# One layer's top-k search: two query tiles searched one by one, first query operands made earlier

## The chip, the cores and the metric

The kernel runs on one core of one Trainium2 chip. The time is device microseconds of one execution; the median of three runs before the change is 1343.3 us (1337.26 to 1343.76).

## The reference

One decoder layer for a sequence of 1024 tokens with 1024 channels, in float32. A conditioning vector gives shift, scale and gate; the modulated input is projected into attention (8 heads of 64), an indexer and pooling channels. The part that matters here is the sparse attention: for each query the indexer scores every earlier token, the 256 best are kept, and attention runs over those alone.

```python
logits = einsum('bqhd,bsd->bqhs', iq, ik) * (IDX_DIM ** -0.5)
score = einsum('bqh,bqhs->bqs', w, relu(logits))
score = where(causal, score, -inf)
_, idx = lax.top_k(score, k_sel)            # k_sel = 256
...
s = einsum('bqhd,bqkhd->bhqk', q, kg) * (HEAD_DIM ** -0.5)
p = softmax(where(valid, s, -inf)); o = einsum('bhqk,bqkhd->bqhd', p, vg)
...
x = layer_norm(ALPHA * x + gate1 * (concat([attn, pool_out]) @ w_o))
x = layer_norm(ALPHA * x + gate2 * swiglu(x * (1 + scale2) + shift2))
```

## The kernel before

Queries come in 8 tiles of 128; tile i sees 128·(i+1) keys. The stages follow one another: modulation; indexer projections; the score stage (`lg` on PE, `relu` on ACT, weighted sums into `score_X`); a list of 24 `groups` of projections (8 of u, then 8 of k, then 8 of v, one 1024-deep product each); attention; W_o and layer norm; the feed-forward part with products `gu` and `dn`.

Nobody gathers. For tiles 2 to 7 the 256th largest score of each query is found by bisection on the bits of the scores, and all other scores get a large negative bias in `score_X`, which attention adds. (Tiles 0 and 1 have at most 256 keys and need no search.) `bisect(tiles, cols, on_act)` is that search as a generator of small pieces: a count and a rewriting of the scores into 16-bit `keys` on DVE; 15 steps on the high bits; a middle part on DVE; 16 steps on the low bits; then a final part on DVE (equality, count, a scan that settles ties, and the bias), of some ten instructions per tile, after which the tile is `biased`. On ACT a step is one pass per tile (`ACTIVATE junk…<-keys…,cols…`, a Sign with a sum over the row, and an `ACTIVATION_READ_ACCUMULATOR`), and then four small instructions on POOL on the columns `cols`, which hold one value per query and tile: they make the next candidate, for all tiles of the search at once. The next pass of that search waits for them.

The work order is written by the program: each engine's `Queue` (line 158 is its call, so nearly all rows have that line) keeps a planned clock, and before it issues an instruction `fill` puts search pieces in front of it, as long as a piece ends, on that clock, within `SLACK[queue]` us behind the time at which the instruction could start. Streams opened earlier come first. While `pinned` holds, the order of DVE, ACT and POOL is kept as written. ACT searches `TILES_A`, tiles 3 and 2 as one stream and 7 and 6 as another; DVE searches tiles 5 and 4.

Attention goes by head groups g (0 to 3), pairs of heads, and in each pair tile 2g+1 and then 2g. For a tile `q_make` turns the roped queries (loaded back by `q_load` into `qraw`, transposed on PE as `qT`) into operands in the buffer `qab`: four ACT copies and two DVE subtractions, for a high and a low part. A unit is: scores `s` on PE into one of two PSUM buffers (`psB`), on DVE the bias and row maximum (the custom instruction, `sm_H<-s,score_X`, printed as `ISA` in the orders below), the exponential on ACT, the normalising on POOL, transposes `pT` on PE, copies of those on ACT and DVE, and `o` on PE. The exponential loads an ACT table once (`ACT_TABLE_LOAD`). The buffer areas of SBUF have one letter each (X, V, W, H, T, C, K, R), which ends every name in the profile: `qab_H` lies in area H. V holds values and the pooling data.

Of the kernel before, what the change touches and what calls it, by code (L numbers as in the profile page):

```python
# [12 lines left out]
F32R = mybir.dt.float32r  # L13
# [20 lines left out]
BIG = 1.0e30  # L34
NEG = -3.0e38
NOT_TAKEN = -(2.0 ** 100)
TILES_A = ([3, 2], [7, 6])
TILES_V = [5, 4]
PIN = "VAG"
W_POOL = (1, 3)  # L40
# [7 lines left out]
MODS = (12, 2)  # L48
Q_AT = (((0, 0), (1, 0)), ((0, 0), (1, 0)), ((1, 0), (2, 0)))
WARM = 66  # L50
SLACK = {"V": 0.5, "A": 1.5}
SYNC = 0.06
UPDATE = "G"
POOL_AT = 3
# [123 lines left out]
def decoder_layer_kernel(  # L178
# [22 lines left out]
    def buf(where, off, n, name, dt=F32):  # L201
        return nc.alloc_sbuf_tensor_at(f"{name}_{where}{off}", [P, n], dt, offset=area[where] + 4 * off).ap()
# [59 lines left out]
    def raw_slot():  # L262
        n_raw[0] += 1
        return RAW[(n_raw[0] - 1) % 3]
# [286 lines left out]
    def q_transpose(src):  # L551
        pt = psA("qT")
        for pr in range(4):
            T.transpose(pt[:, pr * P : (pr + 1) * P], src[:, pr * P : (pr + 1) * P], ident)
        return pt
# [56 lines left out]

    kA = buf("X", 4224, 448, "keysA")
    colsA = buf("X", 4672, 128, "colsA")
    junk7 = buf("X", 4800, 512, "junk").bitcast(BF16)
    kD = buf("T", 0, 960, "keysD")
    k4 = buf("T", 960, 320, "keys4")
    k5 = buf("T", 1280, 384, "keys5")
    junkA = buf("X", 6528, 512, "junkA").bitcast(BF16)
    junkB = buf("X", 7040, 256, "junkB").bitcast(BF16)  # L620
    colsD = buf("X", 8576, 64, "colsD")
    keys = {2: kA[:, 0:192], 3: kA[:, 192:448], 4: k4, 5: k5, 6: kD[:, 0:448], 7: kD[:, 448:960]}
    keys = {i: kw.bitcast(I16) for i, kw in keys.items()}
# [3 lines left out]
    def bisect(tiles, cols, on_act):  # L627
# [3 lines left out]
        cntc, kp, sg, cand, pr, M, ng, th, ib, thr, ahead = (col(q) for q in range(11))  # L631
        flip = ib.bitcast(I16)[:, 0:nt]
        kv = {i: keys[i] for i in tiles}
        own = (junkA if 7 in tiles else junkB) if on_act else junk7

        def trash(i):
            return own[:, 0 : P * (i + 1)]
# [100 lines left out]
    def open_stream(*a):  # L738
        pinned.update(PIN)
        b = bisect(*a)  # L740
        streams.append([T.t, next(b), b])
        times.fill = fill
# [40 lines left out]
    for i in range(2, NT):  # L783
        if i == 4:
            open_stream(TILES_A[0], colsA[:, 0:64], True)
        n = P * (i + 1)
        qa, ql = iq_ops(i)
        sc = score(i)
        for pr in range(4):
            pe, po = psB("lg"), psB("lg")  # L790
            scores_pair(pe, po, qa, ql, pr, ikE, ikO, n)
            q_piece()
            if pr == 1 and i + 1 < NT:
                nxt = q_transpose(iq_raw(i + 1))
            for e, pp in ((0, pe), (1, po)):
                h = 2 * pr + e
                rr = rrr[:, (n_rr[0] % 4) * 1024 : (n_rr[0] % 4) * 1024 + n]
                n_rr[0] += 1
                A.activation(rr, pp[:, 0:n], AF.Relu, scale=0.125)
                w1 = wq8[:, i * 8 + h : i * 8 + h + 1]  # L800
                if h == 0:
                    V.tensor_scalar(sc, rr, w1, 0.0, ALU.mult, ALU.add)
                else:
                    V.scalar_tensor_tensor(sc, rr, w1, sc, ALU.mult, ALU.add)
            next(gate_steps, None)
            if pr == 1 and i + 1 < NT:
                q_operands(nxt, *iq_ops(i + 1))
            if pr == 2 and qpend:
                q_flush(1)
                q_evac(*qpend.pop(0))  # L810
        dg = sc[:, n - P : n]
        G.affine_select(dg, dg, pattern=[[-1, P]], compare_op=ALU.is_ge, fill=NEG, base=0, channel_multiplier=1)
    open_stream(TILES_V, colsD, False)
    open_stream(TILES_A[1], colsA[:, 64:128], True)


    SP.dma_start(pscale, pscale_in)
# [90 lines left out]
    def at_(slot, f):  # L908
        late.setdefault(slot, []).append(f)
# [27 lines left out]

    PAIRS = (0, 6, 8, 14, 16)
    held, pair = {}, None
    for n_, (kind, a, b) in enumerate(groups):  # L940
        if n_ in PAIRS:
            pb = psB("pair")
# [26 lines left out]
            at_(nd, lambda a=a, pp=pp: v_take(a, pp))  # L969
        if n_ == 20:  # L970
            at_(n_, lambda: gate_fin(GR, macc, 0, raw_slot()))
        for f in late.pop(n_, []):
            f()
    last = len(groups)
    pinned.clear()


    stat = [buf("X", 8448, 128, "stat")]
# [4 lines left out]
        n_st[0] = (o + n) % 128 if o + n + n <= 128 else 0  # L983
        return stat[0][:, o : o + n]

    ptb = [[buf("H", (2 * s_ + e) * 2048, 2048, "pT").rearrange("p (j q) -> p j q", j=8) for e in (0, 1)] for s_ in (0, 1)]
    smr = buf("H", 8192, 6144, "sm")
    qabh = buf("H", 14336, 1536, "qab", F32R)
    qabw = [buf("W", 6144 - 2048 * i, 1536, "qab", F32R) for i in (0, 1)]
    qabv = [buf("V", 5120 + i * 1536, 1536, "qab", F32R) for i in (0, 1)]  # L990
    qab = {1: qabh, 0: qabw[0], 3: qabw[1], 2: qabw[0], 5: qabh, 4: qabv[0], 7: qabv[1], 6: qabh}

    qops = {}

    qraw = [buf("C", 768, 512, "qraw"), buf("X", 7552, 512, "qraw")]

    def q_load(i):
        raw = qraw[i % 2]
        SP.dma_start(raw, q_d[i])
        return raw  # L1000

    def q_make(i, raw, pt=None):
        b = qab[i]
        qops[i] = (b[:, 0:1024], b[:, 1024:1536])
        q_operands(pt if pt is not None else q_transpose(raw), *qops[i])

    for s_ in (last, last + 1):
        if s_ == last:
            qr = {i: q_load(i) for i in (1, 0)}
            qp = {i: q_transpose(qr[i]) for i in (1, 0)}  # L1010
        for f in late.pop(s_, []):
            f()
    assert not late, late
    for i in (1, 0):
        q_make(i, qr[i], qp[i])

    def cat_slot(g):
        return WS[g]
# [581 lines left out]
```

## Time and profile before

| | |
|---|---|
| three runs | 1343.76, 1343.3, 1337.26 us |
| profiled execution | 1340.45 us, of it the span 1338.5 us |
| mean granted TensorE clock | 0.95 |
| busy | PE 91%, DVE 75%, POOL 45%, ACT 44% |
| stages, roughly | scores to 186 us, projections 186 to 343, attention 343 to 570, W_o and feed-forward to the end |

A row of the timeline is: start, duration, engine, line, operation, out<-in, shapes, xcount of consecutive ones, and in brackets the idle time before it with what released it. A row of the waits is: who waited for whom, us in total, times, longest. A row of grouped instructions is: line, engine, operation, out<-in, shapes, xcount, then total us and mean ns of one, then the idle time before them with its releasers.

### The profile page before, as it was taken

To read this page: it belongs to the slowest core of one execution; us is meant where nothing else is said; L and a number is where in the kernel's file an instruction comes from. 1 tells how busy PE (TensorE), PEld (TensorE's weight loads), DVE (VectorE), ACT (ScalarE), POOL (GpSimd) and SP (SyncE) were. 2 spreads that over 40 slices of the span, in tenths; PEclk is the share of its full clock that TensorE was granted. 3 is DMA by queue.
4 is the path that set the end of the run, shared out by engine and by line. 5 is a ranking of instruction groups with operands and counts; after the bars stand their busy time and mean duration, and the time that the engine had idled before them with its cause. 6 is when DMAs were issued, how large, how long until landed. Compare 5 with 4: busy or idle time off the path is not lost. (4 is left out here: it accounts for less than half of the span.)

```text
span 1338.5 us, 15961 instructions
## 1 busy us (share of the span) xinstructions
PE 1219.7 (91%) x5570; PEld 958.7 (72%) x5570; DVE 1006.4 (75%) x1685; ACT 592.4 (44%) x1103; POOL 606.0 (45%) x624
## 2 busy tenths in 40 slices
PE   7978997989586849999799999999999999999996
PEld 6655676768454526788677888888888888888875
DVE  6898789889766778467887767576767767676688
ACT  2345754667888956427533223232323223232321
POOL 1393584675344536315663414152342414242557
PEclk8999999989677978999899999999999999999998
DMA  9540020221103431420121011120101112110112
GB/s 337 213 162 31 16 92 19 95 68 44 48 24 118 142 111 64 169 84 1 47 79 63 32 63 63 50 76 33 63 32 64 42 53 70 57 63 32 63 48 110
DMA packets 24997, 101.79 MB, mean 76 GB/s; under 512 B 3411, under 2 KB 3411, under 8 KB 20566
## 3 DMA queue, kind: packets, MB, share of 16 engines
q1 hardware_dynamic: 24918, 100.78, 21.5%
q8 instruction: 44, 0.72, 0.2%
q14 instruction: 35, 0.29, 0.1%
HBM read 92.38 MB, written 8.40 MB: 75 GB/s over the span
## 5 line engine op out<-in xcount | busy, mean ns | idle before, releaser
L158 POOL TENSOR_TENSOR wraw_R<-wraw_R 128x512 f32<-128x512 f32 x44 | 60.1, 1366 | 178.3 <-DVE wblk_T L158 51.3
L158 POOL TENSOR_TENSOR wraw_W<-wraw_W 128x512 f32<-128x512 f32 x44 | 59.5, 1353 | 169.3 <-DVE wblk_V L158 63.8
L158 DVE TENSOR_TENSOR res_X<-res_X,dn 128x512 f32<-128x512 f32 (+1 forms) x145 | 97.4, 680 | 50.9 <-PE dn L158 50.9
L158 PE MATMUL gu<-hr_H,wblk_T 128*128 128x512 f32 (+1 forms) x552 | 125.7, 384 | 3.4 <-ACT stage_W L158 2.6
L158 PE MATMUL gu<-hr_H,wblk_V 128*128 128x512 f32 (+1 forms) x552 | 125.5, 382 | 3.3 <-ACT gtmp_V L158 1.8
L158 PE MATMUL gu<-hr_H,wblk_W 128*128 128x512 f32 (+1 forms) x552 | 125.4, 383 | 0.0
L158 PE MATMUL pj<-ws_W,hT_H 128*128 128x512 f32 x456 | 117.9, 406 | 2.4 <-DVE const_C L158 1.6
L158 PEld LDWEIGHTS gu<-hr_H,wblk_T 128*128 128x128 f32 x552 | 101.7, 191 | 23.7 <-ACT stage_W L158 2.9
L158 PEld LDWEIGHTS gu<-hr_H,wblk_V 128*128 128x128 f32 x552 | 101.0, 189 | 24.0 <-ACT gtmp_V L158 2.0
L158 PEld LDWEIGHTS gu<-hr_H,wblk_W 128*128 128x128 f32 x552 | 101.8, 191 | 19.6
L158 PEld LDWEIGHTS pj<-ws_W,hT_H 128*128 128x128 f32 x456 | 84.5, 191 | 27.6 <-issue 10.2
L158 DVE TENSOR_TENSOR utmp_X<-utmp_X,gu 128x512 f32<-128x512 f32 x88 | 58.2, 682 | 33.5 <-PE gu L158 32.4
L158 DVE TENSOR_TENSOR gtmp_V<-gtmp_V,gu 128x512 f32<-128x512 f32 (+1 forms) x96 | 59.1, 638 | 28.2 <-PE gu L158 28.2
L158 POOL TENSOR_TENSOR colsA_X<-colsA_X 128x2 f32<-128x2 f32 x124 | 40.0, 323 | 80.6 <-ACT junkA_X L158 52.4
L158 POOL TENSOR_SCALAR sm_H<-sm_H,stat_X 128x256 f32<-128x256 f32 (+7 forms) x64 | 53.3, 846 | 50.6 <-DVE stat_X L158 40.1
L158 PE MATMUL dn<-wblk_T,act_W 128*128 128x512 f32 (+1 forms) x294 | 75.1, 385 | 0.0
L158 ACT ACTIVATE junkA_X<-keysD_T,colsA_X 128x1024 bf16<-128x1024 uint16 (+3 forms) x62 | 67.7, 1091 | 15.5 <-POOL colsA_X L158 15.1
L158 PE MATMUL dn<-wblk_V,act_W 128*128 128x512 f32 x288 | 74.4, 389 | 0.0
L158 ACT ACTIVATE act_W<-gtmp_V 128x512 fp32r<-128x512 f32 x40 | 25.3, 633 | 94.9 <-DVE gtmp_V L158 92.9
L158 PE MATMUL gu<-hr_H,wblk_R 128*128 128x512 f32 (+1 forms) x276 | 64.1, 381 | 3.4 <-DVE hr_H L158 3.0
L158 DVE TENSOR_SCALAR_CACHE_REDUCE junk_X<-keys_T,colsD_X 128x768 int16<-128x768 int16 (+1 forms) x64 | 64.3, 1005 | 2.0
L158 PEld LDWEIGHTS dn<-wblk_T,act_W 128*128 128x128 f32 x294 | 54.6, 188 | 11.1
(276 smaller groups left out, 2869.6 us busy)
## 6 DMA issues: line engine op xcount, KB each, us to landing
wm_K<-in_wma_dram SPq DMA_DIRECT2D x16, 512.0 KB, 9.6
raw_R<-in_wmc_dram SPq DMA_DIRECT2D x16, 512.0 KB, 3.7
wraw_R<-in_wg_dram SPq DMA_DIRECT2D x6, 1024.0 KB, 4.7
wraw_R<-in_wd_dram SPq DMA_DIRECT2D x6, 1024.0 KB, 4.8
wraw_W<-in_wup_dram SPq DMA_DIRECT2D x6, 1024.0 KB, 4.8
wraw_R<-in_wup_dram SPq DMA_DIRECT2D x5, 1024.0 KB, 4.8
wraw_W<-in_wg_dram SPq DMA_DIRECT2D x5, 1024.0 KB, 4.8
wraw_W<-in_wd_dram SPq DMA_DIRECT2D x5, 1024.0 KB, 4.8
```

Of the source, the lines that this page charges most:

```text
L158: ins_ = f(*a, **k)
```

## The change

- Tiles 7 and 6 are no longer one ACT search of two columns but two searches, tile 6's opened ahead of tile 7's, and both ahead of DVE's. Each has its own `cols` (tile 7's is `colsE_T`), its own `junk`, and four POOL instructions per step of its own.
- ACT's slack is 0.3 us up to the end of the score stage, 2.5 from there to the end of the projections, and 0.3 behind it; it was 1.5 all along.
- The queries of tile 1 are loaded at group 17 and made into operands behind group 20, those of tile 0 at 21 and behind 23, both into area V. Before, they were loaded, transposed and made behind the last group, into H and W. The other tiles' places in H, W and V change with them.

```diff
--- before.py
+++ after.py
@@ -34,7 +34,7 @@
 BIG = 1.0e30
 NEG = -3.0e38
 NOT_TAKEN = -(2.0 ** 100)
-TILES_A = ([3, 2], [7, 6])
+TILES_A = ([3, 2], [6], [7])
 TILES_V = [5, 4]
 PIN = "VAG"
 W_POOL = (1, 3)
@@ -48,7 +48,7 @@
 MODS = (12, 2)
 Q_AT = (((0, 0), (1, 0)), ((0, 0), (1, 0)), ((1, 0), (2, 0)))
 WARM = 66
-SLACK = {"V": 0.5, "A": 1.5}
+SLACK = {"V": 0.5, "A": 0.3}
 SYNC = 0.06
 UPDATE = "G"
 POOL_AT = 3
@@ -612,12 +612,12 @@
 
     kA = buf("X", 4224, 448, "keysA")
     colsA = buf("X", 4672, 128, "colsA")
-    junk7 = buf("X", 4800, 512, "junk").bitcast(BF16)
+    junks = {2: buf("X", 5184, 256, "junk"), 4: buf("X", 4800, 384, "junk"), 6: buf("X", 7040, 448, "junk"),
+             7: buf("X", 6528, 512, "junk")}
...
-    junkA = buf("X", 6528, 512, "junkA").bitcast(BF16)
-    junkB = buf("X", 7040, 256, "junkB").bitcast(BF16)
+    colsE = buf("T", 1664, 64, "colsE")
     colsD = buf("X", 8576, 64, "colsD")
     keys = {2: kA[:, 0:192], 3: kA[:, 192:448], 4: k4, 5: k5, 6: kD[:, 0:448], 7: kD[:, 448:960]}
     keys = {i: kw.bitcast(I16) for i, kw in keys.items()}
@@ -631,7 +631,7 @@
         cntc, kp, sg, cand, pr, M, ng, th, ib, thr, ahead = (col(q) for q in range(11))
         flip = ib.bitcast(I16)[:, 0:nt]
         kv = {i: keys[i] for i in tiles}
-        own = (junkA if 7 in tiles else junkB) if on_act else junk7
+        own = junks[min(tiles)].bitcast(BF16)
 
         def trash(i):
             return own[:, 0 : P * (i + 1)]
@@ -810,8 +810,10 @@
                 q_evac(*qpend.pop(0))
         dg = sc[:, n - P : n]
         G.affine_select(dg, dg, pattern=[[-1, P]], compare_op=ALU.is_ge, fill=NEG, base=0, channel_multiplier=1)
+    SLACK["A"] = 2.5
+    open_stream(TILES_A[1], colsA[:, 64:128], True)
+    open_stream(TILES_A[2], colsE, True)
     open_stream(TILES_V, colsD, False)
-    open_stream(TILES_A[1], colsA[:, 64:128], True)
 
 
     SP.dma_start(pscale, pscale_in)
@@ -937,6 +939,28 @@
 
     PAIRS = (0, 6, 8, 14, 16)
     held, pair = {}, None
+    qr = {}
+    ptb = [[buf("H", (2 * s_ + e) * 2048, 2048, "pT").rearrange("p (j q) -> p j q", j=8) for e in (0, 1)] for s_ in (0, 1)]
+    smr = buf("H", 8192, 6144, "sm")
+    qabh = buf("H", 14336, 1536, "qab", F32R)
+    qabw = buf("W", 6144, 1536, "qab", F32R)
+    qabv = [buf("V", 5120 + i * 1536, 1536, "qab", F32R) for i in (0, 1)]
+    qab = {1: qabv[0], 0: qabv[1], 3: qabh, 2: qabw, 5: qabv[0], 4: qabv[1], 7: qabh, 6: qabv[0]}
+
+    qops = {}
+
+    qraw = [buf("X", 5504, 512, "qraw"), buf("X", 7552, 512, "qraw")]
+
+    def q_load(i):
+        raw = qraw[i % 2]
+        SP.dma_start(raw, q_d[i])
+        return raw
+
+    def q_make(i, raw, pt=None):
+        b = qab[i]
+        qops[i] = (b[:, 0:1024], b[:, 1024:1536])
+        q_operands(pt if pt is not None else q_transpose(raw), *qops[i])
+
     for n_, (kind, a, b) in enumerate(groups):
         if n_ in PAIRS:
             pb = psB("pair")
@@ -969,10 +993,17 @@
             at_(nd, lambda a=a, pp=pp: v_take(a, pp))
         if n_ == 20:
             at_(n_, lambda: gate_fin(GR, macc, 0, raw_slot()))
+        if n_ == 17:
+            qr[1] = q_load(1)
+        elif n_ == 21:
+            qr[0] = q_load(0)
         for f in late.pop(n_, []):
             f()
+        if n_ in (20, 23):
+            q_make(n_ == 20, qr.pop(n_ == 20))
     last = len(groups)
     pinned.clear()
+    SLACK["A"] = 0.3
 
 
     stat = [buf("X", 8448, 128, "stat")]
@@ -983,36 +1014,10 @@
         n_st[0] = (o + n) % 128 if o + n + n <= 128 else 0
         return stat[0][:, o : o + n]
 
...
-    qabw = [buf("W", 6144 - 2048 * i, 1536, "qab", F32R) for i in (0, 1)]
-    qabv = [buf("V", 5120 + i * 1536, 1536, "qab", F32R) for i in (0, 1)]
-    qab = {1: qabh, 0: qabw[0], 3: qabw[1], 2: qabw[0], 5: qabh, 4: qabv[0], 7: qabv[1], 6: qabh}
-
-    qraw = [buf("C", 768, 512, "qraw"), buf("X", 7552, 512, "qraw")]
-
...
     for s_ in (last, last + 1):
-        if s_ == last:
-            qr = {i: q_load(i) for i in (1, 0)}
-            qp = {i: q_transpose(qr[i]) for i in (1, 0)}
         for f in late.pop(s_, []):
             f()
     assert not late, late
-    for i in (1, 0):
-        q_make(i, qr[i], qp[i])
 
     def cat_slot(g):
         return WS[g]
```

In the orders a row is line, operation, out<-in (a name, its area and a buffer number) and tile; the engine is told ahead of each.

ACT, from the last value copies (`vf_V`) to the table load, before: `junkA` are passes of tiles 7 (1024 keys) and 6 (896), `junkB` those of 3 and 2.

```order
L158 ACTIVATE vf_V_1257<-pj_2417 128x512
L158 ACTIVATE junkB_X_612,colsA_X_606<-keysA_X_605,colsA_X_606 128x384
L158 ACTIVATE qab_H_2461<-qT_2470 64x4x128 x4
L158 ACTIVATE qab_W_2462<-qT_2479 64x4x128 x4
L158 ACTIVATE junkA_X_611,colsA_X_606<-keysD_T_608,colsA_X_606 128x1024
L158 ACTIVATE junkA_X_611,colsA_X_606<-keysD_T_608,colsA_X_606 128x896
L158 ACTIVATE junkA_X_611,colsA_X_606<-keysD_T_608,colsA_X_606 128x1024
L158 ACT_TABLE_LOAD
L158 ACTIVATE sm_H_2460,stat_X_2455<-sm_H_2460,stat_X_2455 128x256 x2
```

The same place after the change; `junk_X_609` are tile 6's passes and `junk_X_610` tile 7's, `qab_V_1324` the operands of tile 0.

```order
L158 ACTIVATE junk_X_609,colsA_X_606<-keysD_T_611,colsA_X_606 128x896
L158 ACTIVATE junk_X_610,colsE_T_614<-keysD_T_611,colsE_T_614 128x1024
L158 ACTIVATE vf_V_1223<-pj_2550 128x512
L158 ACTIVATE qab_V_1324<-qT_2577 64x4x128
L158 ACTIVATE junk_X_610,colsE_T_614<-keysD_T_611,colsE_T_614 128x1024
L158 ACTIVATE qab_V_1324<-qT_2577 64x4x128
L158 ACTIVATE junk_X_610,colsE_T_614<-keysD_T_611,colsE_T_614 128x1024
L158 ACTIVATE qab_V_1324<-qT_2577 64x4x128
L158 ACTIVATE junk_X_610,colsE_T_614<-keysD_T_611,colsE_T_614 128x1024
L158 ACTIVATE qab_V_1324<-qT_2577 64x4x128
L158 ACT_TABLE_LOAD
L158 ACTIVATE sm_H_1320,stat_X_2650<-sm_H_1320,stat_X_2650 128x256
```

The copies for tile 1 have gone from here (they stand 18 rows up, among tile 3's and 2's passes), and the four of tile 0 alternate with three passes of tile 7.

DVE at the end of the search, before, from the first row of the pass that belongs to tile 6's final part (the count against the threshold) to tile 6's first use of its bias; `ISA sm_H` is that use, the bias and row maximum, and tile 7's second use stands in between.

```order
L158 TENSOR_SCALAR junkA_X_611,colsA_X_606<-score_X_77,colsA_X_606 128x896
L158 ISA sm_H_2460,stat_X_2455<-s_3495,score_X_77 128x1024
L158 ISA stat_X_2455 128x1
L158 TENSOR_SCALAR colsA_X_606<-colsA_X_606 128x1
L158 SCALAR_TENSOR_TENSOR score_X_77<-keysD_T_608,colsA_X_606 128x896
L158 TENSOR_SCALAR score_X_77<-score_X_77 128x896
L158 RECIPROCAL stat_X_2455<-stat_X_2455 128x2
L158 TENSOR_TENSOR keysD_T_608<-keysD_T_608,score_X_77 128x896
L158 TENSOR_TENSOR junkA_X_611<-junkA_X_611,keysD_T_608 128x896
L158 TENSOR_SCALAR score_X_77<-junkA_X_611 128x896
L158 ISA sm_H_2460,stat_X_2455<-s_3592,score_X_77 128x896
```

DVE at the same place after the change:

```order
L158 SCALAR_TENSOR_TENSOR score_X_77<-keysD_T_611,colsE_T_614 128x1024
L158 TENSOR_SCALAR score_X_77<-score_X_77 128x1024
L158 TENSOR_TENSOR keysD_T_611<-keysD_T_611,score_X_77 128x1024
L158 TENSOR_TENSOR junk_X_610<-junk_X_610,keysD_T_611 128x1024
L158 TENSOR_SCALAR score_X_77<-junk_X_610 128x1024
L158 ISA sm_H_1320,stat_X_2650<-s_3589,score_X_77 128x1024
L158 ISA stat_X_2650 128x1
L158 ISA sm_H_1320,stat_X_2650<-s_3590,score_X_77 128x1024
L158 ISA stat_X_2650 128x1
L158 RECIPROCAL stat_X_2650<-stat_X_2650 128x2
L158 ISA sm_H_1320,stat_X_2650<-s_3733,score_X_77 128x896
```

Tile 6's final part (scan, multiplication, maximum, bias) no longer stands between tile 7's uses and tile 6's own; its rows are now some fifty to ninety rows up, in the third head group.

POOL among the key projections, before: three instructions on `rope_V` are the rope of one key tile, the small ones with 128x2 are an update of one search step.

```order
L158 TENSOR_TENSOR colsA_X_606<-colsA_X_606 128x2
L158 TENSOR_SCALAR colsA_X_606<-colsA_X_606 128x2
L158 TENSOR_TENSOR colsA_X_606<-colsA_X_606 128x2
L158 TENSOR_SCALAR colsA_X_606<-colsA_X_606 128x2
L158 TENSOR_TENSOR colsA_X_606<-colsA_X_606 128x2
L158 TENSOR_SCALAR colsA_X_606<-colsA_X_606 128x2
L158 TENSOR_TENSOR colsA_X_606<-colsA_X_606 128x2
L158 TENSOR_SCALAR colsA_X_606<-colsA_X_606 128x2
L158 TENSOR_TENSOR ptmp_C_457<-rope_V_454,gr_G_76 128x512
L158 TENSOR_TENSOR rope_V_454<-rope_V_454,gr_G_76 128x512
L158 TENSOR_TENSOR rope_V_454<-rope_V_454,ptmp_C_457 128x512
```

POOL there after the change, where 128x1 are tile 6's and tile 7's updates:

```order
L158 TENSOR_TENSOR colsA_X_606<-colsA_X_606 128x2
L158 TENSOR_SCALAR colsA_X_606<-colsA_X_606 128x2
L158 TENSOR_TENSOR colsA_X_606<-colsA_X_606 128x2
L158 TENSOR_SCALAR colsA_X_606<-colsA_X_606 128x2
L158 TENSOR_TENSOR colsA_X_606<-colsA_X_606 128x1
L158 TENSOR_SCALAR colsA_X_606<-colsA_X_606 128x1
L158 TENSOR_TENSOR colsA_X_606<-colsA_X_606 128x1
L158 TENSOR_SCALAR colsA_X_606<-colsA_X_606 128x1
L158 TENSOR_TENSOR colsE_T_614<-colsE_T_614 128x1
L158 TENSOR_SCALAR colsE_T_614<-colsE_T_614 128x1
L158 TENSOR_TENSOR colsE_T_614<-colsE_T_614 128x1
L158 TENSOR_SCALAR colsE_T_614<-colsE_T_614 128x1
```

Between two ropes there are now three updates where there were two; the third is tile 7's own.

More of the change, by code (lines that the diff above doesn't have):

```diff
@@ L984, in stat_cols @@
         return stat[0][:, o : o + n]
-    ptb = [[buf("H", (2 * s_ + e) * 2048, 2048, "pT").rearrange("p (j q) -> p j q", j=8) for e in (0, 1)] for s_ in (0, 1)]
-    smr = buf("H", 8192, 6144, "sm")
-    qabh = buf("H", 14336, 1536, "qab", F32R)
-    qabw = [buf("W", 6144 - 2048 * i, 1536, "qab", F32R) for i in (0, 1)]
-    qabv = [buf("V", 5120 + i * 1536, 1536, "qab", F32R) for i in (0, 1)]
-    qab = {1: qabh, 0: qabw[0], 3: qabw[1], 2: qabw[0], 5: qabh, 4: qabv[0], 7: qabv[1], 6: qabh}
-    qops = {}
-    qraw = [buf("C", 768, 512, "qraw"), buf("X", 7552, 512, "qraw")]
[L997 to L1005, printed above, removed]
     for s_ in (last, last + 1):
-        if s_ == last:
-            qr = {i: q_load(i) for i in (1, 0)}
-            qp = {i: q_transpose(qr[i]) for i in (1, 0)}
         for f in late.pop(s_, []):
```

## The prediction

> **What bounds the kernel now.** I read the table of windows first, because the mean of a whole run hides which stage is short of what, then PE's waits, then the rows around the two longest of them. The columns of a window are the busy time of PE, weight loads, DVE, ACT and POOL, the granted clock, the DMA share and GB/s.
>
> ```profile
> PE 45%; DVE 1%; issue 0%; ACT 0%; DVEq 0%; ACTq 0%
> ...
> 350.00:400.00 50.00, 37.78 (x150) 24.08 (x152) 33.30 (x120) 43.70 (x116) 18.51 (x52) 0.65 0.06 18
> 400.00:450.00 50.00, 34.62 (x197) 22.32 (x194) 32.08 (x74) 43.12 (x91) 25.19 (x50) 0.80 0.41 127
> 450.00:500.00 50.00, 30.21 (x179) 18.87 (x178) 36.65 (x67) 34.54 (x71) 20.53 (x37) 0.84 0.38 127
> ...
> PE s L158 <- DVE stat_X L158: 19.9, 11, 11.1
> PE s L158 <- ACT qab_H L158: 10.6, 1, 10.6
> ```
>
> The chain of waits is PE alone over its last 45%, which is the feed-forward part; the change does not touch it, so time gained or lost before it should reach the end unchanged. From 350 to 450 us, the first half of attention, ACT is the fullest engine (about 43.5 of 50) and PE is below 38. In 450 to 500 no engine is above 37: there something waits in series. PE's two long waits lie at the two ends of this stretch, and the change is aimed at both of them. The first is the start of attention (PE rows, then ACT rows):
>
> ```profile
> 328.74 14.22 PE L158 MATMUL pj<-ws_W,hT_H 128*128 128x512 f32 x62
> 354.41 1.20 PE L158 MATMUL s<-kr_K,qab_H 128*128 128x256 f32 x2 [10.58 <-ACT qab_H L158]
> ...
> 351.50 0.57 ACT L158 ACTIVATE vf_V<-pj 128x512 f32<-128x512 f32 x1
> 352.58 2.40 ACT L158 ACTIVATE qab_H<-qT 64x512 fp32r<-64x512 f32 x4
> 355.00 2.41 ACT L158 ACTIVATE qab_W<-qT 64x512 fp32r<-64x512 f32 x4
> 361.86 1.28 ACT L158 ACT_TABLE_LOAD   x1
> 363.16 0.51 ACT L158 ACTIVATE sm_H<-sm_H,stat_X 128x256 f32<-128x256 f32 x1
> ```
>
> PE's last value projection ends at 342.96, but ACT takes its result only at 351.50. ACT is behind by 8.5 us with search passes, then makes the query operands, and its first exponential is at 363.16. The second place is the end of the search (ACT, DVE, PE):
>
> ```profile
> 485.71 1.04 ACT L158 ACTIVATE junkA_X<-keysD_T,colsA_X 128x896 bf16<-128x896 uint16 x1
> ...
> 492.44 0.68 DVE L158 TENSOR_SCALAR keysD_T<-score_X,colsA_X 128x896 bf16<-128x896 f32 x1
> 498.25 1.22 DVE L158 CUSTOM_DVE_ANT_0 sm_H<-s,score_X 128x1024 f32<-128x1024 f32 x1
> 501.79 2.08 DVE L158 TENSOR_TENSOR_SCAN score_X<-keysD_T,colsA_X 128x896 bf16<-128x896 bf16 x1
> 505.00 1.42 DVE L158 TENSOR_TENSOR junkA_X<-junkA_X,keysD_T 128x896 bf16<-128x896 bf16 x1
> 508.03 1.09 DVE L158 CUSTOM_DVE_ANT_0 sm_H<-s,score_X 128x896 f32<-128x896 f32 x1
> ...
> 499.54 4.37 PE L158 MATMUL s<-kr_K,qab_H 128*128 128x512 f32 x8 [11.07 <-DVE stat_X L158]
> 506.00 3.67 PE L158 MATMUL pT<-const_C,sm_H 128*128 128x128 f32 x16 [2.10 <-POOL sm_H L158]
> 524.45 1.97 PE L158 MATMUL pT<-const_C,sm_H 128*128 128x128 f32 x16
> 536.00 1.78 PE L158 MATMUL pT<-const_C,sm_H 128*128 128x128 f32 x14
> ```
>
> The last pass of the joint search ends at 486.75. Both tiles' final parts then stand on DVE, first tile 7's (its use at 498.25), then tile 6's (508.03). The first pair of heads takes 506.00 to 524.45, 18.45 us, the next one 11.55.
>
> **The change, term by term.** Sums are against the profiled execution's 1340.45 us (span 1338.5 and 1.95 around it).
>
> *Score stage.* The lower slack keeps search passes from standing ahead of ACT's relus.
>
> ```profile
> 130.85 0.62 PE L158 MATMUL lg<-ikE_K,qa_K 128*128 128x512 f32 x2 [3.50 <-ACT relu_K L158]
> ```
>
> That wait can go: −3.5. In return the count and key rewriting of tiles 6 and 7 move ahead of the weight splits on DVE, one share each. The end is bounded by +3, somewhat under the wait itself; I take −2, nearer to the removed wait, which is a row, than to the added one, which is none.
>
> *Key projections.* One joint update of two columns becomes two updates, each of four POOL instructions; over the whole search that is 31 steps more. Nine of them stand between the third and the last key rope. The windows' row is for that stretch:
>
> ```profile
> 263.00:319.00 56.00, 51.33 (x226) 41.32 (x225) 51.17 (x101) 32.98 (x64) 43.81 (x64) 0.94 0.21 66
> ...
> L158 POOL TENSOR_SCALAR colsA_X<-colsA_X 128x2 f32<-128x2 f32 x120 | 40.4, 337 | 10.6
> L158 POOL TENSOR_TENSOR colsA_X<-colsA_X 128x2 f32<-128x2 f32 x124 | 40.0, 323 | 80.6 <-ACT junkA_X L158 52.4 <-ACT junkB_X L158 22.8
> ```
>
> A step is 2 × 0.337 + 2 × 0.323 = 1.32 us, so nine are 11.9, and POOL is idle for 56 − 43.8 = 12.2: they just fit. Between 0 (they fit) and +6 (half of them come ahead of a rope that PE waits for) I take +1. The two query loads, the transposes and tile 1's four ACT copies, which move into this and the value phase, cost nothing: ACT has 23 us free in that window, DMA is busy for 0.21, and the eight transposes are only carried out earlier. If ACT were full there, the copies' 2.4 us would be added.
>
> *Start of attention.* Before, 361.86 − 352.07 = 9.8 us lie on ACT between its last value copy and the table load. Now four query copies (2.4) and three passes of tile 7 (1.15 + 0.10 each with their accumulator read, 3.75), 6.2 us, and some 0.7 of waits for updates: −2.9. Tile 1's operands exist before, so PE can start its scores at once. Of the 8.5 us by which ACT is late I take 3 away, because three streams fill the waits that two left, while three more passes stand ahead. So −6, between 0 (ACT is late as before and later by the three passes) and −11 (the lag goes too).
>
> *Attention until the search ends.* ACT's rows between 361.8 and 487 us, and its one large wait there:
>
> ```profile
> L158 ACT ACTIVATE junkA_X<-keysD_T,colsA_X 128x1024 bf16<-128x1024 uint16 x16 | 18.4, 1148 | 7.0 <-POOL colsA_X L158 7.0
> L158 ACT ACTIVATE junkA_X<-keysD_T,colsA_X 128x896 bf16<-128x896 uint16 x16 | 16.5, 1033 | 0.0
> L158 ACT ACTIVATE pT_H<-pT 128x512 f32<-128x512 f32 x24 | 13.9, 592 | 0.9 <-PE pT L158 0.9
> L158 ACT ACTIVATE sm_H<-sm_H,stat_X 128x768 f32<-128x768 f32 x8 | 7.4, 926 | 0.0
> L158 ACT ACTIVATE sm_H<-sm_H,stat_X 128x640 f32<-128x640 f32 x8 | 6.6, 824 | 0.6 <-DVE stat_X L158 0.6
> L158 ACT ACTIVATE qab_V<-qT 64x512 fp32r<-64x512 f32 x8 | 4.7, 589 | 0.1
> L158 ACT ACTIVATE ws_W<-o 128x256 fp32r<-128x256 f32 x11 | 4.2, 379 | 3.5 <-PE o L158 3.4
> ...
> ACT junkA_X L158 <- POOL colsA_X L158: 7.9, 7, 3.4
> ```
>
> ACT is the bound, so passes count in full. 37 passes stand behind the table load before and 34 now: −3 × 1.24 = −3.7. A joint search offers two independent passes to each wait; tile 7's last 16 steps are one chain. In ACT's new order six pairs of them stand with next to nothing between, so waits of a step's 1.32 us, some 8, take the place of 7.9; with updates that other POOL work delays I add 2.2. Net −1.5, between −3.7 and +4.
>
> *End of the search.* Tile 6's final part moves into the third head group. Of tile 7's part only the 0.68 row disappears. Behind it, tile 6's first use needs PE's scores, which end at 499.54 + 4.37 = 503.9, and not 508.03: −4.1 at least; at most the pair's 18.45 − 11.55 = 6.9. The middle, 5.5, and the 0.7 make −6, between −3 (DVE's third group, with about 10 us of tile 6's work, delays ACT) and −7.6.
>
> Sum: −2 + 1 − 6 − 1.5 − 6 = −14.5, so 1326 for a profiled run like this one. The median of the runs, 1343.3, is 2.9 above it; I add half of that: **1327**. About 0.5%, 6.7 us, is what a measurement of this kernel tells from no change.
>
> **A rule against the extra updates.** In two rows that end together, POOL's small update lasts 1.74 us, though its mean is 0.32, while DVE scans:
>
> ```profile
> 338.08 1.74 POOL L158 TENSOR_TENSOR colsA_X<-colsA_X 128x2 f32<-128x2 f32 x1
> ...
> 338.01 1.82 DVE L158 TENSOR_TENSOR_SCAN score_X<-keys_T,colsD_X 128x768 bf16<-128x768 bf16 x1
> ```
>
> The Trainium skill, SBUF — State Buffer, section "SBUF: two separate sides", says that DVE and GpSimd share one pair of ports as an exclusive lock: a GpSimd instruction that meets a DVE instruction with two SBUF inputs is held for all of that instruction. The trace agrees, with 1.74 beside 1.82. Taken as it stands, the rule has tile 6's final part, moved among tile 7's updates, hold POOL for its scan and its two two-input instructions.
>
> **Rivals.**
>
> A. *Tile 7's chain ends last.* Its 16 low steps stand among ACT work of 14 × 0.59 (transposes) + 6 × 0.92 and 4 × 1.02 (exponentials with their reads) + 8 × 0.59 (queries) + 11 × at most 0.38 = 26.8, and 16 × 1.25 = 20 for the passes: 47 us. The chain alone is 16 × (1.25 + 1.32) = 41. It decides from an update of 1.7 us on. If half of the updates hold one stretched instruction (1.74 in place of 0.32), their mean is 2.03 and the chain 52.5: +5.7. With the scan's 2.08 once more on it, +8: 1335. For it: the row of 1.74, and four passes that nearly touch at the end. Against it: six microseconds of room. The lock rule above is one way to it.
>
> B. *Slower: ACT's slack of 2.5 in the projections.* It allows a pass to delay a weight split or an evacuation by 1.0 us more than before, and PE already shows such a wait:
>
> ```profile
> 230.96 0.51 PE L158 MATMUL pair<-ws_W,hT_H 128*128 128x512 f32 x1 [4.27 <-ACT ws_W L158]
> ```
>
> With 24 groups, all hit in full, that is +24: 1351. It takes more than 21 us (0.9 per group) to end slower than before. Against it: PE is busy for 51.3 of 56 us in the window above, and an evacuation delayed by 1 us has a second buffer behind it.
>
> C. *The start gains nothing.* ACT is as far behind at its last value copy as the three extra passes make it (3.7 us later), and that eats the rest. Then 6 us are missing: 1333. For it: 8.5 us of lag now.
>
> D. *Everything at its good end.* −3.5 + 0 − 11 − 3.7 − 7.6 = −25.8: 1316.
>
> That the change does not do what it says is excluded by ACT's and DVE's new order, where tile 6's final part stands ahead of tile 7's end.
>
> **Chances.** My forecast 0.42, A 0.20, C 0.15, B 0.13, D 0.10. The forecast's own range is 1319 to 1335. The range 1312 to 1342 takes in A, C and D and leaves out B and the outer tails, under 2 in 10. Faster by over 0.5%, below 1336.6: 0.40 of the forecast, half of A, 0.12 of C, all of D, 0.72. Within 0.5%: 0.02 + 0.10 + 0.03 + 0.02 of B, 0.17. Slower: the rest of B, 0.11.
>
> **What would show it.** No wait of PE's `lg` on relu above 1 us; `kT` waits under 3 us in all; first exponential near 355; search passes end near 478 and ACT's wait for `cols` below 12 us; tile 6's use of its scores within 6 us of tile 7's; pairs of heads 12 us apart from the first on. I am wrong if the last pass ends later relative to the first exponential than the 123 us of now, or if the first exponential is not ahead of 360.

## The result, and the profile after

The changed kernel takes 1358.2 us (median of four runs, 1357.33 to 1359.69) against 1341.25 before: 1.3% slower, ratio 1.013 with a 95% interval of 1.010 to 1.0161. The forecast was 1327, and its range ended at 1342. The profiled execution took 1357.33 us, 16.9 more than the one of before.

The windows of attention after the change (columns as before: PE, weight loads, DVE, ACT, POOL, granted clock, DMA):

```profile
350.00:400.00 50.00, 36.15 (x148) 22.93 (x147) 32.57 (x120) 39.88 (x107) 24.22 (x74) 0.66 0.06 17
400.00:450.00 50.00, 35.73 (x197) 23.42 (x197) 37.34 (x89) 39.07 (x85) 31.64 (x66) 0.77 0.39 118
450.00:500.00 50.00, 38.75 (x194) 23.46 (x190) 31.14 (x59) 34.57 (x69) 26.76 (x52) 0.79 0.45 146
500.00:550.00 50.00, 36.10 (x170) 21.83 (x172) 29.57 (x55) 23.32 (x44) 21.68 (x22) 0.69 0.11 32
```

ACT, which was the fullest engine with 43.5 of 50, is now at 39.5, and no other engine has taken its place: something waits in series from 350 us on, and to 550 where it had been to 500. PE's waits, the ones that answer to those shown before and the new ones:

```profile
PE s L158 <- DVE stat_X L158: 28.4, 10, 15.1
PE pj L158 <- DVE gr_G L158: 5.1, 1, 5.1
PE kT L158 <- DVE colsD_X L158: 4.2, 1, 4.2
PE s L158 <- ACT qab_V L158: 4.1, 1, 4.1
```

The start of attention after the change (PE, then ACT):

```profile
332.59 19.32 PE L158 MATMUL pj<-ws_W,hT_H 128*128 128x512 f32 x72 [5.07 <-DVE gr_G L158]
352.10 0.80 PE L158 MATMUL s<-kr_K,qab_V 128*128 128x256 f32 x4
...
351.94 0.60 ACT L158 ACTIVATE vf_V<-pj 128x512 f32<-128x512 f32 x1 [1.25 <-PE pj L158]
359.35 1.28 ACT L158 ACT_TABLE_LOAD   x1
360.64 0.51 ACT L158 ACTIVATE sm_H<-sm_H,stat_X 128x256 f32<-128x256 f32 x1
```

ACT is no longer late at the last value copy, and PE starts its scores at once. But PE's last projection itself ends at 351.9, where it ended at 342.96, so the first exponential gains 2.5 us and not the 7 that the forecast's three terms ahead of it come to (−2 + 1 − 6).

The end of the search after the change (ACT, POOL, DVE, PE):

```profile
499.10 1.14 ACT L158 ACTIVATE junk_X<-keysD_T,colsE_T 128x1024 bf16<-128x1024 uint16 x1
501.22 1.15 ACT L158 ACTIVATE junk_X<-keysD_T,colsE_T 128x1024 bf16<-128x1024 uint16 x1 [0.89 <-POOL colsE_T L158]
...
501.54 2.34 POOL L158 TENSOR_TENSOR raw_R<-raw_R,gr_G 128x1024 f32<-128x1024 f32 x1
...
512.61 1.23 DVE L158 CUSTOM_DVE_ANT_0 sm_H<-s,score_X 128x1024 f32<-128x1024 f32 x1
517.55 1.09 DVE L158 CUSTOM_DVE_ANT_0 sm_H<-s,score_X 128x896 f32<-128x896 f32 x1 [1.08 <-PE s L158]
...
513.90 3.92 PE L158 MATMUL s<-kr_K,qab_V 128*128 128x512 f32 x8 [15.12 <-DVE stat_X L158]
539.67 1.97 PE L158 MATMUL pT<-const_C,sm_H 128*128 128x128 f32 x16
551.21 1.78 PE L158 MATMUL pT<-const_C,sm_H 128*128 128x128 f32 x14
```

The last pass ends at 502.4, 15.6 us later than before. (POOL is then at work on `raw_R` until 503.9, and the search's last update waits for that.) Tile 6 follows tile 7 within 5 us on DVE (517.55 against 512.61; it was 9.8), as forecast, and still the second pair's transposes come 25.8 us after PE's first scores, where it was 24.9.

Three times split each execution: the first exponential, the end of the last search pass, and the start of W_o's high part, the long `wo<-hr_H` row (568.82 before). Behind that the two traces are alike (771.6 and 772.2 us to the end).

| kernel (profiled execution) | first exponential | to the last pass | to W_o |
|---|---|---|---|
| before | 363.2 | 123.6 | 82.1 |
| after | 360.6 | 141.7 | 82.7 |

So −2.5, +18.1 and +0.6 are the 16.9 us, with 0.6 behind. The net loss is all in the time that the search takes beside attention. Ahead of the first exponential a larger gain and a larger loss nearly cancel; they are taken apart in the account of the prediction below.

### The profile page after: what moved, and what is told of

Read it like the earlier page. It is cut to its first block, busy times and chain, and to the rows that moved or that the text cites. A ratio compares the mean times of both kernels' runs of the same rounds, so it can differ in the third digit from the quotient of the medians.

```text
span 1355.4 us, 16113 instructions
## 1 busy us (share of the span) xinstructions
PE 1232.8 (91%) x5570; PEld 966.1 (71%) x5570; DVE 1003.3 (74%) x1700; ACT 593.1 (44%) x1103; POOL 634.1 (47%) x746
## 5 line engine op out<-in xcount | busy, mean ns | idle before, releaser
L158 PE MATMUL pj<-ws_W,hT_H 128*128 128x512 f32 x456 | 120.9, 413 | 8.2 <-DVE gr_G L158 5.1
L158 PE MATMUL gu<-hr_H,wblk_V 128*128 128x512 f32 (+1 forms) x552 | 125.2, 381 | 2.5 <-ACT gtmp_V L158 1.8
L158 PE MATMUL dn<-wblk_V,act_W 128*128 128x512 f32 x288 | 74.4, 389 | 0.0
L158 PE MATMUL s<-kr_K,qab_V 64*128 64x512 f32 (+7 forms) x128 | 39.9, 462 | 34.1 <-DVE stat_X L158 26.4
L158 PEld LDWEIGHTS dn<-wblk_T,act_W 128*128 128x128 f32 x294 | 54.6, 188 | 11.1
L158 PE MATMUL dn<-wblk_W,act_W 128*128 128x512 f32 x240 | 62.2, 389 | 0.0
```

The source lines that it names most:

```text
L158: ins_ = f(*a, **k)
```

## The experiments

Fifteen kernels were run in four lots. Medians are the kernel's; ratios are to the kernel before in the same lot, with their 95% intervals.

### The change taken apart

Joint search again, all else as changed:

```diff
-TILES_A = ([3, 2], [6], [7])
+TILES_A = ([3, 2], [7, 6])
-        own = junks[min(tiles)].bitcast(BF16)
+        own = junks[7 if 7 in tiles else min(tiles)].bitcast(BF16)
-    open_stream(TILES_A[2], colsE, True)
```

> The changed kernel with tiles 7 and 6 searched as one stream again; slacks, early query operands and the late opening of DVE's search stay as changed. Theory A (the split: tile 7's last low steps form one dependent chain at the end, and 31 more updates stand on POOL): the search end goes back by about 15 us and the time to 1340 to 1346. Theory S (the slack of 0.3 us behind the projections leaves search steps to the end, whoever they belong to): the end is as late as now, 1353 to 1360. In the projections, if the extra updates on POOL make the time lost there, the last value projection ends near 335; if the late opening of DVE's search does, it stays near 345.

Slack 1.5 all through, split kept (the two lines that set `SLACK["A"]` later are taken out):

```diff
-SLACK = {"V": 0.5, "A": 0.3}
+SLACK = {"V": 0.5, "A": 1.5}
```

> The changed kernel with ACT's slack 1.5 all through, as before; split and early operands stay. In ACT's order tile 7's search then ends about 60 rows earlier, ahead of the last head group. Theory S: faster than the changed kernel by 15 or more, 1335 to 1343. Theory A in its form of extra updates on POOL: the cost stays, 1352 to 1360. The score stage should lose the 8 us that the changed kernel won there.

The early operands alone (the first two edits together, and DVE's stream opened ahead of ACT's):

> The kernel before with only the query operands of tiles 1 and 0 made early (joint search, slack 1.5, DVE's search opened first). If making them early is worth what was forecast of the start of attention, 3 to 6 us less than before, 1335 to 1338; if ACT is late anyway, 1341 as before.

The split alone, in the kernel before (its `TILES_A`, `junks` and `colsE` put into it, 6 opened ahead of 7):

> The kernel before with only the split of tiles 7 and 6 (slack 1.5, DVE's search first, operands late). Theory A: slower than before by 10 or more, 1351 up. Theory S: not slower than before by over 3; with tile 6's final part out of the end, 1332 to 1341.

| kernel | median us | ratio | first exponential | to the last pass | to W_o |
|---|---|---|---|---|---|
| joint | 1336.76 | 0.997 (0.9953 to 0.9987) | 355.7 | 129.8 | 80.1 |
| slack 1.5 | 1351.87 | 1.0084 (1.0056 to 1.0112) | 359.6 | 82.1 | 140.1 |
| early operands alone | 1337.94 | 0.9973 (0.9954 to 0.9991) | 363.2 | 123.7 | 81.4 |
| split alone | 1353.64 | 1.0096 (1.0063 to 1.0129) | 378.3 | 70.7 | 135.1 |

Both kernels with the split are slower than before, both without it a little faster (by 0.3%, under the 0.5% that the prediction took for the least that can be told, though both intervals leave out 1). So the split makes the loss and the slack alone does not; but the form of theory A that blames the lone steps at the end does not hold for the second and fourth: their search ends long before attention needs it, and time is lost all the same, with the split alone all of it ahead of the first exponential, which comes 15 us late. The joint kernel also speaks against the extra updates as the cause of the lost lead in the projections: its last value projection ends at 350.4.

### Round trips or added work

A step of a search is a pass on ACT, an update on POOL, and then the next pass. I took each step's rows apart (from the start of a pass to the start of the next one of the same search; the update counts up to its third instruction, which makes the candidate):

| search, the steps counted | steps | one step | passes (with what stands between) | wait in POOL's queue | update | wait for ACT |
|---|---|---|---|---|---|---|
| before, 7 and 6 jointly | 19 | 6.69 | 3.93 | 0.16 | 1.17 | 1.42 |
| after, tile 6 | 15 | 4.65 | 1.14 | 0.85 | 1.00 | 1.67 |
| after, tile 7 | 16 | 4.74 | 1.25 | 0.44 | 1.13 | 1.91 |

The steps counted before run from 357.3 to 484.4, 127 us. One of them, from 360.6 to 384.5, is 23.9 us long, because the table load and the first exponentials and copies of attention stand between its two passes in ACT's order; the other 18 average 5.7. After the change tile 6's steps run from 365.7 to 435.5 (70 us) and tile 7's from 425.5 to 501.2 (76 us). They stand one behind the other but for 10 us, because the planner serves tile 6 first, and take 135.5 us from end to end. That is 8.4 us more than before. They also begin 5.1 us behind the first exponential, where they had begun 5.8 ahead of it. Together, less 1.2 for the shorter last step, this is the 18.1 us. One step of tile 7, ACT and POOL:

```profile
446.00 1.14 ACT L158 ACTIVATE junk_X<-keysD_T,colsE_T 128x1024 bf16<-128x1024 uint16 x1
449.70 1.15 ACT L158 ACTIVATE junk_X<-keysD_T,colsE_T 128x1024 bf16<-128x1024 uint16 x1 [2.47 <-POOL colsE_T L158]
...
446.47 2.45 POOL L158 TENSOR_SCALAR sm_H<-sm_H,stat_X 128x640 f32<-128x640 f32 x2 [1.95 <-DVE stat_X L158]
448.89 0.19 POOL L158 TENSOR_TENSOR colsE_T<-colsE_T 128x1 f32<-128x1 f32 x1
```

The pass is over at 447.1; POOL has just begun to normalise two rows for attention, and the update waits behind them until 448.89; ACT, with nothing else ahead in its order, stands idle for 2.5 us. What ACT's passes of tiles 6 and 7 waited for from 350 us on, after the change:

```profile
ACT junk_X L158 <- POOL colsE_T L158: 11.5, 11, 2.5
ACT junk_X L158 <- POOL colsA_X L158: 4.7, 4, 1.7
ACT junk_X L158 <- DVE colsA_X L158: 4.4, 1, 4.4
```

The waits for POOL's updates are the first two, 16.2 us together, where they were 7.9; the third is one wait of tile 6 for its middle part on DVE. To test what these waits cost, the passes of tiles 6 and 7 were given a candidate that does not change, so that they wait for nobody; all passes and updates are still made, and the thresholds of these two tiles are not searched for any more:

```diff
+            if free:                       # free = min(tiles) >= 6
+                V.memset(col(15), 0.5 - float(1 << (bits - 1)))
...
-                    A.activation(trash(i), kv[i]..., AF.Sign, bias=one(cand, m), accum_out=one(cntc, m))
+                    cnt_ = col(11 + b % 4) if free else cntc
+                    A.activation(trash(i), kv[i]..., AF.Sign, bias=one(col(15) if free else cand, m), accum_out=one(cnt_, m))
```

> The changed kernel, but the passes of tiles 6 and 7 take a constant candidate and count into four columns in turn, so that a pass no longer waits for the update of the step before; all passes and all POOL updates are still made (the threshold found is then not the right one). Theory C (the loss is the round trips: 31 dependent steps of pass, POOL and back in a row after the table load, 4.7 us each, in place of 19 of 6.7): the search end falls by 12 us or more against the changed kernel and the time to 1338 to 1347. Theory P (the loss is POOL's and ACT's added work itself, the extra updates): it stays within 4 us of 1358.

The same in the kernel before:

> The kernel before with the same edit on its joint search of tiles 7 and 6. Theory C: its 19 round trips have a second pass in each, the gain is smaller than in the split kernel, 2 to 8 us, 1333 to 1339. Theory P: within 3 us of before.

All of ACT's searches in turns:

```diff
-advance(min(todo, key=lambda st: (st[1][0] != "G", streams.index(st))))
+advance(min(todo, key=lambda st: (st[1][0] != "G", st[0] if q.name == "A" else streams.index(st))))
```

> The changed kernel, but ACT's searches take turns (the one whose last piece is oldest goes next) where tile 3's and 2's went first, then 6's, then 7's. Theory C: two chains that alternate cover each other's round trips; faster than the changed kernel by 5 to 15, 1343 to 1353. Theory P: as the changed kernel, 1354 to 1360.

Joint search, with DVE's stream opened first:

> The joint search with the changed slacks and the early operands (as in the first experiment, 1336.8) and DVE's search opened ahead of it as before. If DVE is late in the key projections because its search was opened last, PE's last value projection ends near 343 instead of 350 and the time is 1328 to 1334. If the slack of 2.5 makes it late, 1335 to 1340.

| kernel | median us | ratio | first exponential | to the last pass | to W_o |
|---|---|---|---|---|---|
| split, free of the wait | 1339.72 | 0.9998 (0.9973 to 1.0024) | 358.3 | 123.4 | 81.7 |
| joint, free of the wait | 1329.2 | 0.9914 (0.9889 to 0.9939) | 363.8 | 112.6 | 81.5 |
| searches in turns | 1336.24 | 0.9957 (0.9936 to 0.9978) | 355.0 | 55.3 | 154.5 |
| joint, DVE first | 1367.41 | 1.0194 (1.0177 to 1.0211) | 363.7 | 148.9 | 82.1 |

Without the wait the split kernel is 18.5 us faster than the changed one (their medians are of different lots), the joint one 10.8 faster than before (3 more than I had put as its most). With all searches in turns the changed kernel, with all its 31 added updates, is a little faster than the kernel before, and 7 us under what I had expected of it. So the updates' own work is not the loss; round trips in a row are. They are not shown to be all of it: freed of them, the split kernel still takes 205.1 us from the first exponential to W_o and the joint one 194.1, and the two differ also in slack, early operands and the places of their passes, which no run here takes apart. (The split kernel's profiled execution, 1334.45 us, is 5.3 below its median, so its row in the table flatters it.) What was expected of the last kernel was wrong by far: DVE's stream first makes the last value projection end at 360 instead of 350, and eight joint steps are left to the end, alone on ACT:

```profile
506.96 1.15 ACT L158 ACTIVATE junk_X<-keysD_T,colsA_X 128x1024 bf16<-128x1024 uint16 x1 [0.91 <-POOL colsA_X L158]
510.27 1.15 ACT L158 ACTIVATE junk_X<-keysD_T,colsA_X 128x1024 bf16<-128x1024 uint16 x1 [0.90 <-POOL colsA_X L158]
```

A joint step that nothing else covers costs 3.3 us (510.27 − 506.96), a single one 2.1 (501.22 − 499.10). A split search has to hide its round trips behind other passes, or it pays 4.2 for two.

### Where the steps stand

Tiles 3 and 2 first as before, 6 and 7 in turns (each stream gets a mark, `a[0] != TILES_A[0]`, that is compared ahead of its age):

> The changed kernel with one edit in the planner: tiles 3 and 2 keep their place, and the searches of 6 and 7 take turns where 6 had always gone ahead of 7. In ACT's order both end together, ahead of the last head group, and no passes of tile 7 stand alone at its end. Theory C (two chains in a row cost the round trips twice): 1322 to 1336, ahead of the kernel before. Theory P (the updates' own work): 1350 or more.

The same with a slack of 0.8 behind the projections:

> The last one with a slack of 0.8 behind the projections in place of 0.3, so that passes come earlier and may hold up the attention's exponentials. Theory C: within 6 us of the last one; if passes ahead of the exponentials starve PE, slower by 5 to 10.

The changed kernel with 1.5 there, tile 6 still first:

> The changed kernel with a slack of 1.5 behind the projections alone; tile 6 is still searched ahead of tile 7. ACT's order has the search finished well ahead of the last head group, so the lone passes at the end are gone. If those alone are the loss: 1336 to 1342. If it is the two chains in a row, wherever they stand: 1345 to 1355.

The joint kernel with 1.5 there:

> The joint search with early operands, slack 0.3 in the score stage, 2.5 in the projections and 1.5 behind them. The search ends about 12 rows earlier on ACT than in the first experiment. If the place of the search's end sets the time: 1326 to 1333; if passes ahead of the exponentials cost as much as they bring: 1334 to 1340.

| kernel | median us | ratio | first exponential | to the last pass | to W_o |
|---|---|---|---|---|---|
| 6 and 7 in turns | 1344.69 | 1.0025 (1.0009 to 1.0042) | 364.3 | 115.8 | 92.6 |
| the same, slack 0.8 | 1345.54 | 1.0025 (1.0008 to 1.0041) | 365.5 | 80.9 | 128.9 |
| changed, slack 1.5 behind | 1346.22 | 1.003 (1.001 to 1.0049) | 361.3 | 74.4 | 138.0 |
| joint, slack 1.5 behind | 1333.19 | 0.9921 (0.99 to 0.9943) | 355.5 | 113.2 | 93.5 |

From the first exponential to W_o it is 224.4 us in the changed kernel, 208.4 in turns, 212.4 with the larger slack, 206.7 joint with 1.5 behind, 205.7 before. In turns 16 of the 18.7 us come back. Giving tile 7 its steps earlier, though still behind tile 6, brings 12. The rest of the distance to the joint kernel lies ahead of the first exponential (364.3 against 355.5). About half of it stands behind the last value copy, where the kernel in turns has four passes of 6 and 7 and the joint one has one; the other half is a last value projection that ends at 354.3 for 350.2. I had expected the first of these four ahead of the kernel before; it is 0.25% behind. The last one, joint with early operands and slacks of 0.3, 2.5 and 1.5, beats both kernels of this case.

### The two terms that failed for other reasons

Behind the search PE was given work that nobody reads, held until tile 7's threshold is known:

```diff
                 pair_cat(*units[n_ - 1][0:2], pair_pv(*units[n_ - 1][0:2]))
+                if units[n_ - 1][0:2] == (2, 3):
+                    wt = psA("warm7")
+                    T.transpose(wt[0:1, 0:P], colsE[:, 20:21], ident)
+                    for _ in range(32):
+                        T.transpose(wt[:, 0:P], ident, ident)
```

> The changed kernel with 33 transposes on PE whose result nobody reads, put behind the third head group's last product and held until tile 7's threshold is known, so that PE works in the last 8 us of its wait of 15. If the first pair of heads behind the search is bound by PE's clock: PE's granted clock is 1.00 soon after its scores start, the pair is 6 to 9 us shorter and the time 1349 to 1353. If tile 6's or DVE's work binds it: 1356 to 1361.

> The kernel before with the same 33 transposes in its wait of 11 us. If the clock binds the first pair there: 3 to 6 us faster than before, 1334 to 1338. If tile 6's final part on DVE binds it, as the prediction held (it is on DVE until 508 here): within 2 us of before.

And DVE's search was cut short (`search_v(6, ng, True)` for 16):

> The changed kernel with the low part of DVE's search of tiles 5 and 4 cut from 16 steps to 6 (it leaves the rest of those bits out), about 26 us less on DVE, which is busy for 47.6 of every 50 us between 250 and 350. If DVE's load is what takes the lead of the score stage away, PE's last value projection ends at 335 to 342 instead of 352 and the first exponential is at 345 to 353. If ACT or POOL takes it away, they stay within 3 us.

| kernel | median us | ratio | first exponential | to the last pass | to W_o |
|---|---|---|---|---|---|
| changed, PE kept at work | 1352.09 | 1.0072 (1.0046 to 1.0098) | 359.8 | 143.0 | 78.8 |
| before, PE kept at work | 1340.61 | 0.9987 (0.997 to 1.0004) | 366.6 | 125.2 | 80.9 |
| changed, DVE's search short | 1343.25 | 0.9996 (0.9974 to 1.0018) | 353.4 | 138.7 | 82.6 |

Windows of 4 us behind the search, first before, then after the change:

```profile
504.00:508.00 4.00, 2.00 (x10) 2.00 (x11) 3.81 (x5) 0.60 (x1) 2.85 (x2) 0.50 0.00 0
512.00:516.00 4.00, 3.94 (x13) 1.78 (x12) 3.99 (x7) 2.49 (x4) 2.84 (x2) 1.00 0.00 0
...
520.00:524.00 4.00, 4.00 (x9) 1.82 (x8) 1.23 (x2) 3.33 (x7) 0.00 (x0) 0.50 0.02 4
528.00:532.00 4.00, 4.00 (x8) 1.67 (x7) 1.62 (x3) 1.13 (x2) 3.60 (x4) 0.50 0.44 131
532.00:536.00 4.00, 4.00 (x24) 2.61 (x22) 2.52 (x6) 2.44 (x5) 1.69 (x2) 0.89 0.00 1
```

After the change PE is busy for the whole of these windows, at half its clock, for some 18 us from 513.9 on; the kernel before is back at 1.00 by 512, 12 us behind its first scores. With the stand-in work the changed kernel's pair shrinks (PE's rows):

```profile
506.03 5.19 PE L158 MATMUL warm<-const_C 128*128 128x128 f32 x32
514.33 3.00 PE L158 MATMUL s<-kr_K,qab_V 128*128 128x512 f32 x8 [3.11 <-DVE stat_X L158]
536.15 1.97 PE L158 MATMUL pT<-const_C,sm_H 128*128 128x128 f32 x16
```

It is 21.8 us from the scores to the second pair, for 25.8 (6 to 9 us less had been expected), and the kernel is 6 us faster. In the kernel before it went from 24.9 to 23.8, and the time moved by less than can be measured: there the transposes were over 5 us before the scores began, and the clock had fallen again, so that run settles nothing about the clock before.

DVE's windows in the changed kernel, and the second of them with the short search:

```profile
250.00:300.00 50.00, 38.46 (x159) 30.36 (x158) 47.94 (x93) 32.47 (x64) 42.14 (x73) 0.86 0.18 58
300.00:350.00 50.00, 42.81 (x178) 33.90 (x177) 47.58 (x108) 32.87 (x75) 24.76 (x79) 0.90 0.11 36
...
300.00:350.00 50.00, 43.29 (x195) 34.78 (x193) 35.54 (x78) 37.98 (x83) 29.89 (x91) 0.98 0.13 39
```

With 26 us less on DVE the last value projection ends at 343.7 instead of 351.9 and the first exponential comes 7 us earlier, both just past the late end of what was expected. The key projections do not move (the last `kT` at 316.7 and 316.6), so DVE's load is most of what makes the value phase late, and what holds the key phase stays open. The kernel is 15 us faster than the changed one, but part of the search is left out there, and the same cut was not run in the kernel before.

The early operands have a part in this. PE's row of the last 72 value projections, before and with the early operands alone:

```profile
326.03 16.93 PE L158 MATMUL pj<-ws_W,hT_H 128*128 128x512 f32 x72
...
339.63 19.37 PE L158 MATMUL pj<-ws_W,hT_H 128*128 128x512 f32 x72 [3.00 <-DVE gr_G L158]
```

With the early operands alone PE waits for DVE ahead of tile 1's query transposes (5.4 us for `kr_K`) and behind them (the 3.0 of this row), and its last value projection ends at 359.0, 16 us behind the kernel before. What they save at the start of attention makes up for it: the first exponential is at 363.2 in both. In the four kernels without early operands (before, the split alone, the joint one free of the wait, before with PE kept at work) the last run of projections takes 35.5 to 35.7 us, in all others 38.3 to 50.4, and 38.3 is the one with DVE's search cut short.

## Why the prediction was wrong, point by point

Both signs that it had named for being wrong came: the last pass ends 141.7 us behind the first exponential, not 123 or less, and the first exponential is at 360.6, not ahead of 360. Two of its steps failed by over 10 us each, the first two below.

- **Attention until the search ends**, forecast −1.5 with an upper bound of +4, measured +18.1. This is the step that made the loss. I counted three passes less on ACT, took ACT's occupancy for the bound, and put 8 us of waits in the place of 7.9. I counted the round trips of tile 7's last 16 steps only. Tile 6's 15 steps in front of them are a chain of the same kind, and what had been 19 trips with two passes each became 31 with one. The upper end of the range should have come from a row in which a pass waits for its own update, taken 31 times.
- **Key projections**, forecast +1, with the early operands put at nothing in this and the value phase; measured +16.4 over both: from the start of the run of 96 `pj` behind the first u pairs to the end of the last value projection it is 166.9 us for 150.5. Of these, 5.4 come up to the last `kT` (316.7 for 318.8), within the upper bound of +6, and 11.0 behind it. The third pair of groups still starts 9.9 us ahead (221.1 for 231.0) and the last value projection ends 8.9 behind. This step failed too, and a gain on each side of it hides that. The updates that I had weighed on POOL are not it, since the joint kernel has the same lag. I had costed the early operands there at nothing with ACT's free time as the cover, and did not look at DVE's, which had 4.8 of 56 us: alone they make the last value projection 16 us late, and DVE's shorter search takes 8.2 off.
- **Rival A** named the mechanism and sized it by 8. Its sum had 47 us of ACT work for 16 steps and found six microseconds of room; the 16 steps took 63.4. It left out that a pass that is ready waits 1.9 us for its place in ACT's order, and that an update waits 0.44 behind attention's work on POOL. The lock rule (the Trainium skill, SBUF — State Buffer, section "SBUF: two separate sides"), by which a POOL instruction is held during a DVE instruction with two SBUF inputs, is not what grew: an update takes 1.17 us before and 1.00 and 1.13 after. There are more of them in a row.
- **End of the search**, forecast −6, measured +0.6. The move was made as described, and tile 6's use on DVE came 5 us behind tile 7's. But the long first pair was not tile 6's: from the first scores to the second pair PE is busy nearly throughout in both kernels, and in the changed one at a clock of 0.50. I read 18.45 − 11.55 as a wait and did not look at the clock of those windows. The longer wait ahead of it (15.1 us for 11.1) is one thing that came with it; the run with stand-in work shows that 4 us of that pair hang on the clock.
- **Score stage**, forecast −2 within −3.5 and +3, and it was more: the run of 96 `pj` starts at 185.0 for 192.5, −7.4. The long wait on relu is 0.2 us:

```profile
133.39 0.61 PE L158 MATMUL lg<-ikE_K,qa_K 128*128 128x512 f32 x2 [0.20 <-ACT relu_K L158]
```

- **Start of attention**, forecast −6, measured −11.5: from the last value projection to the first exponential it is 8.7 us for 20.2. ACT's lag of 8.5 us is gone, as forecast in part. But PE's own lateness has taken its place: with the score stage's −7.4 and the projections' +16.4 only −2.5 is left.
- **Rival B** (the slack of 2.5) is not what made the kernel slower, since the joint kernel with that slack is faster than before. Whether it loses the score stage's lead in the key projections is not settled: with 1.5 all through there is no such lead to lose (the run of 96 starts at 193.1), the last value projection still ends at 349.8, and no run has 0.3 in the score stage and 1.5 behind it. The early operands alone are worth 0.3% in all.

What stays open: why the split with slack 1.5 loses its time at other places, ahead of the first exponential when alone and behind the search with early operands; I have only its traces, with ACT late in the one (PE waits 13.4 us for `qab_H`) and PE at 19 of 50 us from 350 to 400 in the other.

## What to carry to other kernels

A search that goes pass, update, pass is a chain of round trips, and its price is the trip's length times its count, whatever the busy shares say: 19 trips of 6.7 us were cheaper than 31 of 4.7, of which only 10 us overlapped. If such a chain is split into two, they have to alternate, so that each covers the other's trip; a planner that serves streams in a fixed order puts them one behind the other. Work that is moved to where one engine has time can still be late on another: early operands looked free on ACT and made PE wait for DVE. Before a slow stretch is put down to a late operand, look at whether its engine was busy and at what clock.

## What the runs showed of the hardware that I had not expected

After a wait of 15.1 us PE worked from 513.9 on with hardly a gap, and its granted clock was still 0.50 at 532, some 18 us on; in the kernel before it was back within 12 us of the first scores. The Trainium skill, TensorE: Matmul & The Clock Gate, section "Part 1: The HAM clock gate", gives a warm-up of about 3.4 us. These two traces show it several times longer. The run with stand-in work agrees with it for the transposes: they begin at 505.9, and the 0.85 of the window from 508 to 512 puts the change to 1.00 at about 509.2, 3.3 us on (an estimate, from a clock that is 0.50 or 1.00). Behind a gap of 3.1 us it fell to 0.50 again at 516, and under the scores and transposes that followed it was still 0.50 at 524. What makes the difference no run here shows. Windows of that run:

```profile
508.00:512.00 4.00, 3.22 (x24) 2.98 (x22) 3.88 (x4) 0.00 (x0) 0.00 (x0) 0.85 0.02 4
512.00:516.00 4.00, 1.67 (x6) 0.89 (x6) 3.71 (x7) 1.69 (x3) 0.00 (x0) 1.00 0.45 131
516.00:520.00 4.00, 4.00 (x9) 1.94 (x8) 2.25 (x6) 2.97 (x6) 1.28 (x2) 0.50 0.00 0
520.00:524.00 4.00, 4.00 (x14) 2.70 (x14) 2.21 (x5) 2.23 (x4) 1.49 (x2) 0.50 0.00 0
```
